# Products of zeros on TensorE while the tokens are chosen: 40 in layer 0, 110 in layer 1

## The chip, the cores and the metric

One core of a Trainium2 chip runs the whole program, so there is one span and one TensorE clock to look at. The metric is device time in microseconds of one execution, the median over several. [...]

## What is computed

Two layers of a diffusion backbone on 1024 latent tokens and, in layer 0, 256 context tokens, 1024 wide, in float32. Each layer has a mixer (windowed attention and spatial gating in layer 0, latent attention and a short convolution in layer 1) and then a feed-forward with 16 experts that choose their tokens:

```python
def expert_choice_ffn(h, w_router, w1, w3, w2):
    n_tok, d = h.shape[1], h.shape[2]
    cap = EC_FACTOR * n_tok // N_EXPERTS
    aff = jax.nn.softmax(jnp.einsum('bnd,de->bne', h, w_router).astype(jnp.float32), axis=-1)
    gate, idx = lax.top_k(jnp.swapaxes(aff, 1, 2), cap)
    xs = jax.vmap(lambda hb, ib: hb[ib])(h, idx)
    a = jnp.einsum('becd,edf->becf', xs, w1)
    b = jnp.einsum('becd,edf->becf', xs, w3)
    y = jnp.einsum('becf,efd->becd', jax.nn.silu(a) * b, w2) * gate[..., None].astype(h.dtype)
```

The choice is a top 128 of 1024 for each expert. No expert can start before the affinities of the last tokens are known, ranked, merged, turned and used to gather rows.

## The kernel before, in words

Every float32 product is three float16 products of high and low halves (`mm3`, L141 to L143). The weights come from memory as 1 MB slabs, `raw`; ScalarE writes the high half (L100) and VectorE the low one (L101) into `spl`.

The mixer of a layer is written as streams that `weave` mixes. Its last stage is `tail`, for 128 tokens at a time: the output projection `yps`, the norm, the router's logits `lg` (L319), a softmax, and a transposition of the affinities into `affps` (L333), which VectorE copies to `aff` (L334).

The choice is `topk` on VectorE: 16 rounds of MAX8, MATCH_REPLACE8 and FIND_INDEX8 (L350, L354, L356) on the last 384 tokens; the first 640 are ranked earlier, beside other work. `merge` joins the two lists (L368 to L372, the last writes `tkir`), `slots` turns indices and gates on TensorE into `slps` (L382, L384), VectorE copies them (L385, L386), and GpSimd's queue then gathers the rows `xs` of expert 0 (L488). In `experts` TensorE transposes `xs` into `tr` (L155), ScalarE and VectorE scale and split them into `xsh` and `xsl`, and the first expert products `pa`, `pb` follow. Ahead of those, TensorE makes two broadcasts of the modulation, `bcps` (L259), and in layer 0 `m5ps` (L509) and the context rows `trc` (L481).

In layer 0, `mods1` runs after the mixer's streams. It makes the first modulation bank of layer 1: nine groups of products `modps` on slabs `mslab`, a VectorE copy of the bank (L212), four transpositions `tr<-mod` and small VectorE operations (L234, L235). It shares the two buffers `za` in PSUM with the last tile of the mixer. A product of zeros is already there: `mod_bank` opens its bank with one (L193), on the tile `zero16`.

A scheduler sets the order of the instructions on every engine: it simulates the program with costs of its own and gives an engine, each time it is free, something that is ready in that simulation. On the chip each engine then goes through its list in that order. `issue_after(ins)` says that what is in it may be placed only after `ins`; it adds no wait of its own on the chip. `high_priority` puts something ahead of what else is ready.

Of the kernel before, what the change touches and what calls it, by code (L numbers as in the profile page):

```python
# [22 lines left out]
P = 128  # L23
# [3 lines left out]
NE = 16  # L27
# [26 lines left out]
def weave(*streams):  # L54


    live = [[st[0], 0.0, float(st[1]), st[2] if len(st) > 2 else 0.0, None] for st in streams]
    while live:
        s = min((v for v in live if v[4] is None or v[4]()), key=lambda v: v[3] + v[1] / v[2])
        try:  # L60
            r = next(s[0])
            s[4] = r if callable(r) else None
            s[1] += 0.0 if callable(r) else r
        except StopIteration:
            live.remove(s)
# [12 lines left out]
class Net:  # L78
# [61 lines left out]
    def mm3(self, ps, lh, ll, rh, rl, first, last):  # L140
        self.T.matmul(ps, lh, rh, start=first, stop=False)  # L141
        self.T.matmul(ps, lh, rl, start=False, stop=False)  # L142
        return self.T.matmul(ps, ll, rh, start=False, stop=last).ins  # L143

    def turn(self, dst, src):

# [136 lines left out]
    def tail(self, l, j, t, src, catT, wout, m2, xd, h2d, aff, psum, c4, t2, cn=None, xin=None, ptr=None):  # L283

        V, S, T = self.V, self.S, self.T
        ra, rb = self.RT[l, j]
        x = xin
        if x is None:
            x = c4([P, D], "xres")
            self.G.dma_start(x, src)  # L290
        for h in range(2):
            ps = psum([P, 512], "yps")
            for k in range(8):
                ch, cl = catT(k)
                wh, wl = wout(k, h)
                self.mm3(ps, ch, cl, wh, wl, k == 0, k == 7)
                if k % 2:
                    yield 1.3
            sl = slice(h * 512, (h + 1) * 512)
            if m2 is None:  # L300
                V.scalar_tensor_tensor(x[:, sl], ps, IS, x[:, sl], op0=OP.mult, op1=OP.add)
            else:
                tmp = t2([P, 512], "ytmp")
                V.tensor_tensor(tmp, ps, m2[:, sl], OP.mult)
                V.tensor_tensor(x[:, sl], x[:, sl], tmp, OP.add)
        self.G.dma_start(xd[t * P:(t + 1) * P, :], x)
        ptr = ptr or psum
        xn = (cn or c4)([P, D], "xn2")
        r = self.stats(x, D, xn, "t")
        hs = []  # L310
        for h in range(2):
            ps, = self.trans(x[:, h * 512:(h + 1) * 512], 4, ptr)
            hT = t2([P, 4, P], "h2T")
            S.activation(hT, ps, AF.Copy)
            hs.append(hT)
            yield 0.5
        lg = ptr([P, NE], "lg")
        for k in range(8):
            T.matmul(lg, hs[k // 4][:, k % 4], ra[:, k], start=(k == 0), stop=(k == 7))  # L319
        e = self.small.tile([P, NE], F32, name="re", bufs=2)  # L320
        V.scalar_tensor_tensor(e, lg, r, rb, op0=OP.mult, op1=OP.add)
        nm = self.small.tile([P, 1], F32, name="rnm", bufs=2)
        V.tensor_reduce(nm, e, axis=AX.X, op=OP.max, negate=True)
        den = self.small.tile([P, 1], F32, name="rden", bufs=2)
        self.last_exp = S.activation(e, e, AF.Exp, bias=nm, accum_out=den).ins
        V.reciprocal(den, den)
        V.tensor_scalar(e, e, den, None, op0=OP.mult)
        pt = ptr([P, P], "affps")
        r0, cols = aff[1](t)
        if r0:  # L330
            T.matmul(pt[r0:r0 + NE, :], e, self.ident, start=True, stop=True, tile_position=(0, r0))
        else:
            T.transpose(pt[:NE, :], e, self.ident)  # L333
        V.tensor_copy(aff[0][r0:r0 + NE, cols], pt[r0:r0 + NE, :])  # L334
        S.activation(xn, x, AF.Copy, scale=r)
        self.G.dma_start(h2d[t * P:(t + 1) * P, :], xn)
        yield 1.0
# [295 lines left out]
    def even(self, xd, xdc, h2d, h2dc, then):  # L633
        nc, tc, V, S, T, G, Y, I = self.nc, self.tc, self.V, self.S, self.T, self.G, self.Y, self.I
        with self.pool("m0") as pm, self.pool("m0p", PSUM) as pp:
            za, zc = Tag(pp, "za", BK0[0]), Tag(pp, "zc", BK0[1])
# [212 lines left out]
            K = {}  # L849

            for t in range(NT):
                lo, hi = max(t - 1, 0), min(t + 1, NT - 1)
                n = hi - lo + 1
# [53 lines left out]
            def mods1():  # L907

                tags = itertools.cycle(range(4))
                pw = then()  # L910
                yield from self.mod_bank(1, 0, zq, lambda shape, name: pw.tile(list(shape), F32, name=name, tag=f"w{next(tags)}", bufs=1), (K["turn"], None), 2048)
                with tc.issue_after(K["turn"]):
                    self.first_slabs(0, 0, 7)
                self.split_first(0, 4, self.last_exp)
                self.mod_AB(1, 1, zq)

            pend = []

# [62 lines left out]
    def odd(self, ms, mw, xs, xsc, xd, h2d, W, then):  # L981
        nc, tc, V, S, T, G, Y, I = self.nc, self.tc, self.V, self.S, self.T, self.G, self.Y, self.I
# [8 lines left out]
        if True:  # L991
# [111 lines left out]
            K = {}  # L1103
# [5 lines left out]
            with self.pool("m1zp", PSUM) as pz:  # L1109
# [57 lines left out]
                if True:  # L1167
# [89 lines left out]
                    def att_all():  # L1257

                        for n in range(8 * NT):
                            t, h = n // 8, n % 8  # L1260
                            pTs = K.pop(("p", t, h))
                            for i in range(len(KB)):
                                pend.append((t, h, i, pTs[i]))
                                for c in SP[i]:
                                    if n + LA < 8 * NT:
                                        score((n + LA) // 8, (n + LA) % 8, c)
                                        yield 0.6
                                if len(pend) > AB[3]:
                                    values()
                                    yield 0.3  # L1270
                            done.add(("h", t, h))
                            if h == 7 - LA and t + 1 < NT:
                                yield after(("q", t + 1))
                        while pend:
                            values()
                        for p in (mt, m1, ap):
                            p.__exit__(None, None, None)
                        then()
                        pools.append(self.pool("m1ap2", PSUM))
                        pq = pools[-1].__enter__()  # L1280
                        K["z"] = Tag(pq, "y", 4), Tag(pq, "tr", 2)
                        self.first_slabs(1, 0, FS)
                        done.add("att")

                    def q_all():
                        for t in range(1, NT):
                            yield after(("h", t - 1, 0))
                            yield from Q(t)
                            done.add(("q", t))
# [35 lines left out]
                    def choose():  # L1325
                        yield after(("c", NR1 // P - 1))
                        aff_t = K["aff"]
                        yield from self.topk(aff_t[:, :NR1], NR1, CAP, "r")
                        yield after(("c", NT - 1))
                        with tc.high_priority():  # L1330
                            yield from self.topk(aff_t[:, NR1:], 1024 - NR1, CAP, "l", NR1, aff_t[:, :1024 - NR1], 1)

                    def splits():
                        yield after("att")
                        for i in range(11):
                            yield lambda: len(self.ahead) > i
                            yield 1.0
                            if i in PL:
                                self.split_first(i, i + 1)
                            else:  # L1340
                                raw, _ = self.ahead[i]
                                sp = self.spl()
                                for h in range(2):
                                    hs = slice(h * 1024, (h + 1) * 1024)
                                    self.split_w(raw[:, hs], sp[:, 0, hs], sp[:, 1, hs])
                                self.ahead[i] = raw, sp

                    weave((Q(0), 4))
                    for h in range(LA):
                        for i in range(3):  # L1350
                            score(0, h, i)
                    weave((self.first(att_all(), HP[0]), 29), (q_all(), 6, 0.1), (tails(), CV), (self.first(choose(), HP[2]), 10, TS), (splits(), SPR, 8.6))
                    with tc.high_priority():
                        r = self.slots(*self.merge(self.tk["r"], self.tk["l"]), CAP, zc, False)
                for p in reversed(pools):
# [126 lines left out]
```

## Time and profile before

| | us |
|---|---|
| median of 3 runs | 2637.35 |
| lowest and highest | 2634.41, 2641.68 |
| the profiled execution's own time | 2632.11 |
| its span, first to last instruction | 2630.0 |
| TensorE (PE) busy, share of the span | 2329.2, 89% |
| VectorE (DVE) busy | 1997.7, 76% |
| ScalarE (ACT) busy | 1696.7, 65% |
| mean granted clock of TensorE | 0.943 |

Times in the rows are microseconds from the span's start. In a timeline a row is: start, busy time, engine, line, operation, tile written and tiles read, shapes, count, and in brackets the engine's idle time before it and what ended it. PEld is TensorE's weight load, which lies beside the products. A product's busy time is longer than its distance to the next one, since products are pipelined. The layer 0 choice of tokens lies between 607 and 636 us, layer 0's experts from 646 to 1330 us, the choice of layer 1 between 1997 and 2025 us, and its experts from 2039 us to the end.

### The profile page before, as it was taken

Reading aid. Unit: us, or ns where it says so; the run is one execution under the profiler, and the core shown is the slowest. Engines: PE = TensorE matmul, PEld = TensorE weight load, DVE = VectorE, ACT = ScalarE, POOL = GpSimd, SP = SyncE. Lnnn points to the kernel's source line nnn. Section 1 sums busy time; section 2 is a strip of 40 time slices with the busy share of each in tenths; the row PEclk is TensorE's granted clock in tenths of the full one; section 3 lists DMA queues with packets and bytes.
Section 4 is the critical chain, followed back from the end, with each engine's and each line's share of the span. In section 5 each row is a group of like instructions: output and inputs, shape, how many; then the busy total and the mean of one; then the engine's idle time right before and its main releaser. Section 6 shows DMA issues by size and latency. Waiting matters only on the chain. (4 is left out here: it accounts for less than half of the span.)

```text
span 2630.0 us, 48132 instructions
## 1 busy us (share of the span) xinstructions
PE 2329.2 (89%) x19023; PEld 1415.0 (54%) x19023; DVE 1997.7 (76%) x3586; ACT 1696.7 (65%) x2748; POOL 320.6 (12%) x196
## 2 busy tenths in 40 slices
PE   6889998867999999999969999978982999999995
PEld 2335555543877778786836555535541444444442
DVE  5546767787887788777848687788796889888887
ACT  4434666535777787777726466567655777777774
POOL 1000000003111111111310000000025011112120
PEclk9999999877999999999989999989985999999998
DMA  8783555548998989888967577788866899999997
GB/s 321 192 213 84 134 104 116 123 126 312 352 337 324 328 328 325 327 320 300 326 187 203 119 143 143 133 151 184 176 175 272 311 364 395 368 360 367 361 363 274
DMA packets 461705, 660.25 MB, mean 251 GB/s; under 512 B 371083, under 2 KB 371387, under 8 KB 410789
## 3 DMA queue, kind: packets, MB, share of 16 engines
q1 hardware_dynamic: 439894, 582.81, 69.7%
q0 software_dynamic: 21584, 74.37, 9.8%
q8 instruction: 149, 2.44, 0.4%
q14 instruction: 78, 0.64, 0.1%
HBM read 525.82 MB, written 41.94 MB: 216 GB/s over the span
## 5 line engine op out<-in xcount | busy, mean ns | idle before, releaser
L101 DVE SCALAR_TENSOR_TENSOR spl<-raw,spl 128x2048 f16<-128x2048 f32 x369 | 834.6, 2285 | 167.3 <-ACT spl L100 166.5
L100 ACT ACTIVATE spl<-raw 128x2048 f16<-128x2048 f32 x369 | 693.5, 1911 | 166.4 <-DMA raw<-in_w 109.5
L141 PE MATMUL pa<-xsh,spl 128*128 128x160 f16 x1024 | 214.6, 233 | 2.3 <-ACT xsh L112 2.3
L143 PE MATMUL pb<-xsh,spl 128*128 128x160 f16 x1024 | 214.6, 233 | 0.5 <-DVE spl L101 0.5
L142 PE MATMUL pa<-xsl,spl 128*128 128x160 f16 x1024 | 214.7, 233 | 0.3 <-DVE xsl L114 0.3
L143 PE MATMUL pa<-xsh,spl 128*128 128x160 f16 x1024 | 214.7, 233 | 0.0
L142 PE MATMUL pb<-xsl,spl 128*128 128x160 f16 x1024 | 214.6, 233 | 0.0
L141 PE MATMUL pb<-xsh,spl 128*128 128x160 f16 x1024 | 214.5, 233 | 0.0
L141 PEld LDWEIGHTS <-spl 128*128 128x128 f16 x2048 | 200.6, 98 | 8.9 <-issue 8.0
L141 PE MATMUL y<-spl,gh 128*128 128x512 f16 x512 | 195.2, 384 | 9.0 <-ACT gh L112 8.4
L143 PEld LDWEIGHTS <-spl 128*128 128x128 f16 x2048 | 200.8, 98 | 1.1 <-DVE spl L101 0.7
L142 PEld LDWEIGHTS <-spl 128*128 128x128 f16 x2048 | 200.8, 98 | 0.3
L143 PE MATMUL y<-spl,gl 128*128 128x512 f16 x512 | 190.1, 386 | 11.4 <-DVE gl L114 11.3
L142 PE MATMUL y<-spl,gh 128*128 128x512 f16 x512 | 195.6, 382 | 1.8 <-DVE spl L101 1.8
L594 POOL DMA_INDIRECT xd<-ysb,idxl x31 | 113.2, 3652 | 532.3 <-DVE ysb L587 508.2
L1218 ACT ACTIVATE pr<-sps,nm 128x512 f32<-128x512 f32 (+1 forms) x192 | 116.7, 611 | 88.3 <-DVE nm L1209 67.7
L141 PE MATMUL po<-vS,pT 128*128 128x64 f16 x976 | 118.0, 198 | 49.1 <-DMA pT<-ps 32.5
L1201 PE MATMUL sps<-kT,qT 128*128 128x512 f16 (+1 forms) x576 | 134.4, 355 | 12.3 <-ACT pr L1218 11.9
L114 DVE TENSOR_TENSOR ps<-pr,ps 128x512 f16<-128x512 f32 (+1 forms) x192 | 112.2, 595 | 38.9 <-ACT ps L112 38.3
L141 PEld LDWEIGHTS <-pT 128*128 128x128 f16 x976 | 92.1, 101 | 82.8 <-DMA pT<-ps 46.5
L1202 DVE TENSOR_REDUCE mx<-sps 128x1 f32<-128x512 f32 (+1 forms) x192 | 112.8, 595 | 26.2 <-PE sps L1201 24.9
L208 PE MATMUL modps<-mslab,cs 128*2 128x512 f32 x384 | 88.5, 690 | 33.6 <-DMA mslab<-in_mod_w 28.7
(431 smaller groups left out, 5883.8 us busy)
## 6 DMA issues: line engine op xcount, KB each, us to landing
raw<-in_w SPq DMA_DIRECT2D x384, 1024.0 KB, 6.8
mslab<-in_mod_w SPq DMA_DIRECT2D x80, 512.0 KB, 4.8
mslab<-in_mod_w SPq DMA_DIRECT2D x8, 1024.0 KB, 8.2
raw<-in_wz SPq DMA_DIRECT2D x12, 512.0 KB, 6.4
raw<-in_wconv SPq DMA_DIRECT2D x24, 256.0 KB, 3.8
xin<-in_x POOLq DMA_DIRECT2D x8, 512.0 KB, 4.8
raw<-in_ev_wo SPq DMA_DIRECT2D x8, 512.0 KB, 6.9
xres<-in_x POOLq DMA_DIRECT2D x8, 512.0 KB, 5.4
```

What stands on the lines that cost most here:

```text
L100: self.S.activation(hi, raw, AF.Copy, scale=scale)
L101: self.V.scalar_tensor_tensor(lo, raw, scale, hi, op0=OP.mult, op1=OP.subtract)
L114: return self.V.tensor_tensor(lo, src, hi, OP.subtract)
L141: self.T.matmul(ps, lh, rh, start=first, stop=False)
L142: self.T.matmul(ps, lh, rl, start=False, stop=False)
L143: return self.T.matmul(ps, ll, rh, start=False, stop=last).ins
L208: T.matmul(ps[c0:c0 + 2], lhs, slab[:rows, g * 512:(g + 1) * 512], start=False, stop=(k == 8), tile_position=(0, c0))
L594: G.indirect_dma_start(out=xd, out_offset=IOA(ap=lat[0][:, e:e + 1], axis=0), in_=ysb, in_offset=None, compute_op=OP.add)
L1201: T.matmul(ps[:, :w], qT[:, 4 * j + h % 4], kT[:, k, c0:c0 + w], start=j == 0, stop=j == 2)
L1202: V.tensor_reduce(mx[:, i:i + 1], ps[:, :w], axis=AX.X, op=OP.max)
L1218: S.activation(pr[:, :w], sp[i][:, :w], AF.Exp, bias=nm, scale=SC1, accum_out=dn[:, i:i + 1])
```

## The change

A new helper, `idle`, writes n products of a 128 x 128 block of zeros with a 128 x 512 block of zeros into one PSUM tile that nobody reads. It may be placed only after the transposition of the last affinities, `last_aff`, which `tail` now keeps.

```diff
+    def idle(self, psum, n, ins):
+
+        ps = psum([P, 512], "idle")
+        with self.tc.issue_after(ins):
+            for i in range(n):
+                self.T.matmul(ps, self.zero16[:, 0:1].broadcast_to([P, P]), self.zero16[:, 0:1].broadcast_to([P, 512]), start=i == 0, stop=i == n - 1)
...
-            T.transpose(pt[:NE, :], e, self.ident)
+            self.last_aff = T.transpose(pt[:NE, :], e, self.ident).ins
...
                 self.split_first(0, 4, self.last_exp)
                 self.mod_AB(1, 1, zq)
+                self.idle(za, 40, self.last_aff)
...
+                    self.idle(K["z"][0], 110, self.last_aff)
                     with tc.high_priority():
                         r = self.slots(*self.merge(self.tk["r"], self.tk["l"]), CAP, zc, False)
```

In layer 0 the call stands at the end of `mods1`, behind the choice in the program's text; in layer 1 it stands just ahead of `merge` and `slots`. Where the products land on TensorE is the scheduler's doing. The lines of the changed kernel are 7 to 9 higher than those of before; L150 is the product of zeros.

**TensorE at the end of layer 0's choice, before.** `mod` is the modulation bank, `tkir` the merged indices, `tkvr` the gates, `xc` and `xs` gathered context and latent rows.

```order
L208 MATMUL modps<-mslab,one_77 2x512 x4
L155 MATMUL tr<-c_ident,mod_6688 128x128 x4
L382 MATMUL slps<-c_ident,tkir 128x16
L384 MATMUL slps<-c_ident,tkvr 128x16
L259 MATMUL bcps<-mod_990,c_ident 128x512 x2
L509 MATMUL m5ps<-mod_990,c_ident 32x512 x2
L481 MATMUL trc<-c_ident,xc 128x32 x8
L155 MATMUL tr<-c_ident,xs 128x128 x12
```

The same place in the changed kernel:

```order
L162 MATMUL tr<-c_ident,mod_6688 128x128 x4
L150 LDWEIGHTS zero_75
L150 MATMUL idle<-zero_75 128x512
...
L389 MATMUL slps<-c_ident,tkir 128x16
L391 MATMUL slps<-c_ident,tkvr 128x16
L150 LDWEIGHTS zero_75
L150 MATMUL idle<-zero_75 128x512
...
L266 MATMUL bcps<-mod_990,c_ident 128x512 x2
L516 MATMUL m5ps<-mod_990,c_ident 32x512 x2
L162 MATMUL tr<-c_ident,xs 128x128 x4
L488 MATMUL trc<-c_ident,xc 128x32 x8
```

Of the 40 products of zeros 19 now stand between the bank's transpositions and `slps`, and 21 between `slps` and `bcps`; `trc` has moved behind the first four transpositions of `xs`. VectorE's list has the same order there in both kernels, with the bank's copy behind the last round of the ranking.

**TensorE at the choice of layer 1, before.** `re` are affinities, `xx` the residual rows.

```order
L155 MATMUL tr<-c_ident,xx 128x128 x8
L319 MATMUL lg<-ra_18928,h2T 128x16 x8
L333 MATMUL affps<-c_ident,re 16x128
L382 MATMUL slps<-c_ident,tkir 128x16
L384 MATMUL slps<-c_ident,tkvr 128x16
```

And in the changed kernel:

```order
L326 MATMUL lg<-ra_18969,h2T 128x16 x8
L340 MATMUL affps<-c_ident,re 16x128
L150 LDWEIGHTS zero_75
L150 MATMUL idle<-zero_75 128x512
...
L389 MATMUL slps<-c_ident,tkir 128x16
L391 MATMUL slps<-c_ident,tkvr 128x16
```

All 110 stand between the last affinities and `slps`.

**SyncE's queue in layer 1's experts, before**: the loads of one expert in the later part of the stage, `w1` and `w3` for the first products, `w2` for the second.

```order
L447 DMA raw_29230<-in_w1 128x2048
L447 DMA raw_29245<-in_w3 128x2048
L447 DMA raw_29235<-in_w1 128x2048
L447 DMA raw_29240<-in_w3 128x2048
L447 DMA raw_29338<-in_w2 128x2048
L447 DMA raw_29343<-in_w2 128x2048
L447 DMA raw_29348<-in_w2 128x2048
L447 DMA raw_29419<-in_w1 128x2048
L447 DMA raw_29353<-in_w2 128x2048
```

And in the changed kernel:

```order
L454 DMA raw_29382<-in_w1 128x2048
L454 DMA raw_29387<-in_w1 128x2048
L454 DMA raw_29397<-in_w3 128x2048
L454 DMA raw_29392<-in_w3 128x2048
L454 DMA raw_29490<-in_w2 128x2048
L454 DMA raw_29495<-in_w2 128x2048
L454 DMA raw_29500<-in_w2 128x2048
L454 DMA raw_29505<-in_w2 128x2048
L454 DMA raw_29571<-in_w1 128x2048
```

Nothing was written for this place; the scheduler's simulation went another way after the added products. The four loads of `w2` now come together, and the two of `w1` ahead of those of `w3`. The scheduler also exchanged neighbours on every engine in layer 1's mixer and experts, and a few in layer 0's experts.

## Rows read from the trace of the kernel before

**Rows 1.** The page's slices: granted clock of TensorE in 40 slices of 65.75 us.
```profile
PEclk9999999877999999999989999989985999999998
```
**Rows 2.** Timeline of layer 0 around the end of its choice.
```profile
633.38 0.67 DVE L212 COPY mod<-modps 128x512 f32<-128x512 f32 x1
634.11 1.12 PE L155 MATMUL tr<-c_ident,mod 128*128 128x128 f32 x4 [6.52 <-DVE mod L212]
...
634.94 0.28 DVE L372 TENSOR_TENSOR tkir<-mg_m,tkil 16x128 f32<-16x128 f32 x1
...
635.28 0.28 PE L382 MATMUL slps<-c_ident,tkir 16*128 16x16 f32 x1
...
635.60 3.78 PE L259 MATMUL bcps<-mod,c_ident 128*128 128x512 f32 x4
...
636.26 0.98 POOL L488 DMA_INDIRECT xs<-h,idxl  x1 [7.37 <-DVE gatel L386]
...
641.00 1.09 PE L155 MATMUL tr<-c_ident,xs 128*128 128x128 f32 x8
...
645.81 0.23 PE L141 MATMUL pa<-xsh,spl 128*128 128x160 f16 x1 [2.32 <-ACT xsh L112]
```
**Rows 3.** Landing of the gathers of xs between 630 and 650 us, from its tile's view.
```profile
DMA to landing us min/median/max: 4.4/5.2/6.1
```
**Rows 4.** Line L193, the products of zeros already there: ns shortest/median/longest, first and last.
```profile
L193 PE MATMUL modps<-zero x6: 376/500/634, 0.9 to 1411.7; 128*128 128x512 f16 x6
```
**Rows 5.** Timeline of layer 1 from the last affinities to the first expert products.
```profile
1996.92 0.37 PE L333 MATMUL affps<-c_ident,re 128*16 128x128 f32 x1 [7.95 <-DVE re L327]
...
2024.93 0.28 PE L382 MATMUL slps<-c_ident,tkir 16*128 16x16 f32 x1 [27.64 <-DVE tkir L372]
...
2025.67 3.49 PE L259 MATMUL bcps<-mod,c_ident 128*128 128x512 f32 x4 [0.35 <-DVE gatel L386]
...
2034.21 1.94 PE L155 MATMUL tr<-c_ident,xs 128*128 128x128 f32 x8 [5.04 <-DMA xs<-h,idxl]
...
2039.10 0.61 PE L141 MATMUL pa<-spl,xsh 128*128 128x512 f16 x1 [2.95 <-ACT xsh L112]
...
2039.93 0.63 PE L141 MATMUL pb<-spl,xsh 128*128 128x512 f16 x1
...
2040.36 0.63 PE L142 MATMUL pb<-spl,xsh 128*128 128x512 f16 x1
...
2042.45 0.38 PE L143 MATMUL pa<-spl,xsl 128*128 128x512 f16 x1
...
2042.67 0.38 PE L141 MATMUL pa<-spl,xsh 128*128 128x512 f16 x1
```
**Rows 6.** Stretches: length, busy of PE, PEld, DVE, ACT, POOL, clock, DMA share, GB/s.
```profile
625.87:639.52 13.65, 7.08 (x20) 2.37 (x14) 9.91 (x40) 7.54 (x5) 4.77 (x4) 0.50 0.70 256
646.35:649.76 3.41, 3.23 (x25) 3.22 (x25) 1.15 (x3) 2.10 (x5) 0.00 (x0) 0.50 0.70 216
2028.75:2032.16 3.41, 0.42 (x1) 0.00 (x0) 0.00 (x0) 0.60 (x1) 3.13 (x2) 1.00 0.85 322
2032.16:2042.40 10.24, 5.24 (x16) 2.77 (x17) 4.07 (x5) 3.69 (x5) 2.85 (x2) 0.50 0.48 159
...
650.00:1320.00 670.00, 655.56 (x7787) 526.83 (x7785) 540.33 (x426) 499.52 (x616) 111.74 (x57) 1.00 0.90 323
```
**Rows 7.** Waits of TensorE between 645 and 1330 us, the longest kind: total us, times, longest.
```profile
PE y L143 <- DVE gl L114: 6.6, 12, 0.7
```
**Rows 8.** The chain that ended last, in layer 1's experts: transpositions of xs, once an expert.
```profile
2234.69 0.87 PE tr L155 x8
...
2266.43 0.87 PE tr L155 x8
...
2439.78 0.87 PE tr L155 x8
...
2477.43 0.87 PE tr L155 x8
```

## The prediction

> **What bounds the kernel now.** I read the clock slices first, to see where TensorE runs at the lower clock. In the page's 40 slices the clock is full nearly everywhere; it dips in layer 0's mixer, at the change of layers (slice 21) and around the choice of layer 1 (slices 30 and 31) [rows 1]. The change is about two of these places, so next I read the timeline around each of them, to see who waits for whom.
>
> In layer 0 VectorE is the bound up to the choice: its copy of the modulation bank starts at 633.38, right behind the ranking, TensorE's transpositions of the bank wait for it and start at 634.11, and the merged indices start at 634.94. TensorE turns the indices at 635.28, so at that moment it is idle by hundredths only: the transpositions end at 634.11 + 1.12 = 635.23. After it come the broadcasts from 635.60, the gather of expert 0's rows issued at 636.26, their transpositions at 641.00, and the first expert products at 645.81 [rows 2]. From there TensorE is the bound: it is busy for 655.56 of 670.0 us, at full clock throughout [rows 6], and its longest kind of wait sums to 6.6 us [rows 7].
>
> In layer 1 the choice is VectorE's alone: the last affinities are done on TensorE at 1996.92 + 0.37 = 1997.29, and it stands idle for 27.64 us until the merged indices come, at 2024.93. Then the broadcasts take 3.49 us, the gathered rows end a wait of 5.04 us at 2034.21, and the first expert products start at 2039.10 [rows 5].
>
> **Layer 1: 110 products of zeros in the gap.** A 128x512 product costs its distance to the next: 2040.36 - 2039.93 = 0.43 us at half clock, 2042.67 - 2042.45 = 0.22 us at full clock [rows 5]. The six products of zeros that are there already last 376 to 634 ns [rows 4], as products of data do at the two clocks (0.38 and 0.63 us, [rows 5]); I take zeros at the same price. Weight loads lie beside the products. The nearest dense run that starts at half clock begins at 2039.10 and is at 0.38 us a product from 2042.45, so 3.3 us; I take that for the zeros, 8 products, and 102 at 0.216: 3.4 + 22.0 = 25.4 us, from 1997.3 to 2022.7. The indices come at 2024.93, so nothing waits; 2.2 us are to spare. The bounds: all at full clock, 23.8 us; all at half clock, 110 x 0.427 = 47.0 us, to 2044.3, which is 19.4 us late.
>
> What does the higher clock bring? The broadcasts get some 1.7 us shorter, but the transpositions behind them wait for the gather, so that gives nothing. The first expert products would gain if the clock lasted until them. The trace of before answers this: the clock stood at 1.00 from 2028.75 to 2032.16, after the broadcasts, and at 0.50 from 2032.16 to 2042.40, while TensorE waited for the gather and the split and then began the products [rows 6]. Zeros ahead of the indices lie before that wait, not in it, so the products start at half clock as now. Layer 1 gives 0; if they did start at full clock, half of 2042.4 - 2039.1 = 3.3 us, 1.7 us, would be gained, and I keep that for the range.
>
> **Layer 0: 19 products ahead of the indices.** These stand behind the bank's transpositions, which end at 635.23, and ahead of the indices' transposition, which was ready at that very moment [rows 2]. Nothing hides them. The clock there is 0.50 from 625.87 to 639.52 [rows 6]. With 3.3 us at half clock, 8 products, and 11 at 0.216, they take 3.4 + 2.4 = 5.8 us (bounds 19 x 0.216 = 4.1 and 19 x 0.427 = 8.1). Indices, copies and the gather's issue are late by that.
>
> **Layer 0: 21 products behind them.** They run while the gather is under way, but the broadcasts and the context's transpositions stand behind them. From 635.60 to 641.00 TensorE had 5.4 us of such work before it turned the rows. At full clock the 3.78 us of broadcasts halve, so 3.5 us remain. The zeros take 21 x 0.216 = 4.5 us. TensorE is then done at 635.6 + 5.8 + 4.5 + 3.5 = 649.4, against 641.00: 8.4 us late. The gather, issued at 636.26 + 5.8 = 642.1 and landing 5.2 us later [rows 3], is there at 647.3, so TensorE decides. Bounds: with the fewest zeros at half clock (4.1) and 2.6 added behind, 6.7 us; with all at half clock, 8.1 + 9.0 = 17.1 us. I take 8.4, as dense runs do raise the clock.
>
> The first products of layer 0's experts then start near 654. They began at half clock: 25 products in the 3.41 us from 646.35 [rows 6], worth 1.7 us if the clock were full. Between the rows' transpositions and the products there is a wait of 2.32 us [rows 2], and in the trace the clock fell in it; I take it to fall again, so 0, and keep 1.7 for the range. Behind, TensorE has no slack but its own waits, 6.6 us for the largest kind in 12 pieces [rows 7], most inside an expert; I let 1 us be absorbed. The stage's delay of 7.4 us passes into layer 1, whose first work needs the sum of all experts.
>
> **What moves besides.** The loads of layer 1's experts are issued in another order, and neighbours change places on all engines there and in its mixer. Nothing is added, so the price is only in waits. The scale is in the chain: an expert takes 2266.43 - 2234.69 = 31.7 us in one part of the stage and 2477.43 - 2439.78 = 37.7 us in another [rows 8], 5.9 us apart by order and waits alone. A gain or a loss of one such expert either way is what I allow in the forecast; the value is 0, since both orders keep the same work on each engine.
>
> **Sum.** 0 (layer 1) + 8.4 - 1 (layer 0) + 0 = 7.4, say 7 us slower. The profiled execution would go from 2632.11 to 2639; its span is 2630.0. That execution is 5.2 us under the median of 2637.35, and the same difference on the median gives **2644 us**, 0.27% slower. A measurement of this kernel can tell some 0.3%, 7.9 us, from no change, so the forecast lies just inside that.
>
> **The rivals.**
> *Zeros don't lift the clock (slower).* If products of zeros left the clock at 0.50, layer 0 would lose the upper bound of 17.1 us, and layer 1's 47.0 us would hold the indices back by 19.4: with 1 us absorbed 35.5 us, 2673. It turns slower from where zeros at half clock fill more than 27.64 us, 65 of them. For it: no row shows a run of zeros. Against: the single ones last as long as other products [rows 4]. [...] Chance 0.08.
> *The order costs more.* Two more experts at 37.7 instead of 31.7, 11.8 us, on top of 7: 2656. Chance 0.10, slower.
> *The clock is kept.* The waits ahead of both layers' first products are too short for the clock to fall, and each layer gains 1.7 us; with zeros at full clock (6.7 instead of 8.4) and 1 us absorbed the sum is 6.7 - 1 - 3.4 = 2.3: 2640, no change. For it: in layer 0 the wait is 2.32 us only. Against: the clock fell in both places now. [...] Chance 0.15.
> *The new order of loads is the better one (faster).* Three experts that now take 37.7 us take 31.7: 17.7 gained, 7 lost, 2626.7. For it: TensorE uses both `w1` before `w3` late in the stage, and the new order brings them so. It decides from 15 us of gain. Chance 0.12, of which 0.10 is faster and 0.02 no change.
>
> **How the numbers follow.** The forecast has 0.55. It lies 1 us inside the bound with some 6 us of the order's scatter around it, so 0.27 is no change and 0.28 slower. No change: 0.27 + 0.15 + 0.02 = 0.44. Slower: 0.28 + 0.08 + 0.10 = 0.46. Faster: 0.10. The range goes from 2633 (the kept clock and one expert's 5.9 us gained) to 2657 (the order's loss); it leaves out the faster rival and the clock that zeros don't lift, 2 in 10.
>
> **What would show it.** In layer 0: `idle` products between the bank's transpositions and `slps`, TensorE busy up to `slps`, and `slps` 5 to 6 us behind the merged indices, which didn't wait before; the first `pa` some 8 us later than now against the choice's end. In layer 1: `slps` ended by the merged indices, not by `idle`, and the first `pa` still at 0.43 us a product. It would be wrong if `slps` of layer 0 came at once, if a clock of 1.00 stood at either first `pa`, or if the stage of layer 1's experts were over 6 us shorter or longer.

## The result, and the profile after

The changed kernel takes 2666.07 us (median of 4 runs, 2661.51 to 2670.05) against 2639.51 of the kernel before on the same chip (4 runs, 2634.41 to 2642.19): a ratio of 1.0093, 95% interval 1.0077 to 1.011, so 20 to 29 us slower. The direction was forecast; the size is over three times the forecast's 7 us, and the time lies 9 us above the range.

The changed kernel's page has the granted clock, in tenths of full speed, in 40 slices of 66.5 us; against [rows 1] only five slices differ: 3 and 4 in layer 0's mixer, and 30 to 32 around layer 1's choice, where slice 31, with the 110 products in it, goes from 5 to 8.

```profile
PEclk9988999877999999999989999989978899999998
```

The timeline of layer 0 around the end of its choice, in the changed kernel (start, us, engine, line, operation, what ended the idle time before):

```profile
637.32 1.12 PE L162 MATMUL tr<-c_ident,mod 128*128 128x128 f32 x4 [5.78 <-DVE mod L219]
...
638.15 0.28 DVE L379 TENSOR_TENSOR tkir<-mg_m,tkil 16x128 f32<-16x128 f32 x1
638.23 6.54 PE L150 MATMUL idle<-zero 128*128 128x512 f16 x19
...
644.70 0.23 PE L389 MATMUL slps<-c_ident,tkir 16*128 16x16 f32 x1
...
644.92 4.76 PE L150 MATMUL idle<-zero 128*128 128x512 f16 x21
645.20 2.28 DVE L101 SCALAR_TENSOR_TENSOR spl<-raw,spl 128x2048 f16<-128x2048 f32 x1
645.48 2.86 POOL L495 DMA_INDIRECT xs<-h,idxl  x1 [13.39 <-DVE gatel L393]
...
654.95 0.65 PE L162 MATMUL tr<-c_ident,xs 128*128 128x128 f32 x4 [2.24 <-DMA xs<-h,idxl]
...
660.98 0.29 PE L141 MATMUL pa<-xsh,spl 128*128 128x160 f16 x1 [3.07 <-ACT xsh L112]
```

The indices are ready at 638.43 and are turned at 644.70: 6.3 us that did not exist before, the 19 products [rows 2]. The 21 behind them take 4.76 us, at the full clock (1.00 from 644.92 to 649.68). But the transpositions of the rows end a wait for the gather, not for TensorE: the gather's issue took 2.86 us instead of 0.98, beside a VectorE split that now falls on the same moment. Two things make it fall there: in the changed order ScalarE's half of that split stands ahead of the copies of the broadcasts, where the old order has it between them, and with the zeros it had long ended (641.25) when `slps` came. Without the zeros the same order has the split at 643.67, clear of the gather's issue at 640.06.

The timeline of layer 1 from the zeros to the first products, changed kernel:

```profile
2031.34 26.23 PE L150 MATMUL idle<-zero 128*128 128x512 f16 x110
...
2056.79 4.06 POOL L441 TENSOR_TENSOR spl<-raw,spl 128x2048 f16<-128x2048 f32 x1 [2.02 <-ACT spl L440]
2057.05 3.94 DVE L375 TENSOR_TENSOR mg_m<-tkvr,tkvl 16x128 f32<-16x128 f32 x1
...
2062.85 0.28 PE L389 MATMUL slps<-c_ident,tkir 16*128 16x16 f32 x1 [5.29 <-DVE tkir L379]
...
2063.59 3.78 PE L266 MATMUL bcps<-mod,c_ident 128*128 128x512 f32 x4 [0.35 <-DVE gatel L393]
2063.73 2.87 POOL L495 DMA_INDIRECT xs<-h,idxl  x1 [2.88 <-DVE gatel L393]
...
2077.46 0.63 PE L141 MATMUL pa<-spl,xsh 128*128 128x512 f16 x1
2077.89 0.63 PE L142 MATMUL pa<-spl,xsh 128*128 128x512 f16 x1
```

The 110 products end at 2057.57 and `slps` waits another 5.29 us for VectorE: they are hidden. In that wait the clock falls again: it is 1.00 up to 2062.70 and 0.50 from 2062.80 to 2075.78. The broadcasts take 3.78 us at 0.50, no better than the 3.49 of [rows 5]; the four of layer 0 take 1.98 at 1.00 (from 649.75). The first products are still 2077.89 - 2077.46 = 0.43 us apart.

So the places that the forecast speaks of carry some 12 us. For the rest I cut the kernel into six stages: layer 0's choice (last affinities to the first `pa`), its experts (to the last `ysb`), layer 1's mixer in two parts (to the first `sps`, with the low-rank projections; then to the last affinities), layer 1's choice, its experts. The windows of the changed kernel (columns as in [rows 6]):

```profile
609.99:660.98 50.99, 33.33 (x149) 10.29 (x150) 32.03 (x102) 27.62 (x29) 22.72 (x9) 0.70 0.67 250
660.98:1350.04 689.06, 674.31 (x7884) 537.43 (x7887) 544.09 (x435) 503.00 (x623) 108.20 (x57) 0.99 0.88 315
1350.04:1527.67 177.63, 148.22 (x1137) 95.09 (x1129) 121.76 (x468) 80.91 (x228) 12.01 (x16) 0.91 0.67 179
1527.67:2031.17 503.50, 439.47 (x3761) 250.24 (x3762) 385.23 (x974) 321.02 (x740) 28.85 (x21) 0.93 0.76 159
2031.17:2075.78 44.61, 32.50 (x125) 14.45 (x126) 33.82 (x91) 22.42 (x17) 29.18 (x9) 0.81 0.61 246
2075.78:2631.93 556.15, 536.05 (x2552) 253.82 (x2552) 481.79 (x311) 430.48 (x411) 83.12 (x29) 0.99 0.97 366
```

The same stages in a second profile of the kernel before, taken later (the first is of an execution 5 us under the median):

```profile
610.77:649.83 39.06, 22.68 (x108) 5.86 (x109) 32.03 (x102) 27.33 (x29) 21.77 (x9) 0.67 0.83 312
649.83:1339.82 689.99, 673.00 (x7884) 536.33 (x7887) 544.57 (x435) 502.47 (x623) 105.15 (x57) 1.00 0.88 316
1339.82:1513.57 173.75, 147.21 (x1136) 94.72 (x1129) 119.88 (x468) 80.95 (x228) 11.30 (x16) 0.92 0.69 184
1513.57:2011.46 497.89, 434.71 (x3761) 248.12 (x3762) 384.89 (x974) 327.51 (x744) 32.96 (x22) 0.93 0.78 167
2011.46:2053.55 42.09, 6.08 (x16) 3.10 (x16) 30.67 (x91) 17.43 (x13) 25.10 (x8) 0.54 0.49 192
2053.55:2616.55 563.00, 539.90 (x2552) 255.06 (x2552) 482.10 (x311) 430.03 (x410) 87.30 (x29) 0.98 0.96 361
```

Stage by stage the change is +11.9, -0.9, +3.9, +5.6, +2.5 and -6.9 us. These sum to 16 us of the 26.6, since this second profile is of an execution 9 us over the median of its runs and the changed kernel's of one 5 us under; against the first profile the stages are +12.0, +3.2, +5.9, +10.0, +2.4 and -7.0. Layer 1's mixer and experts, where nothing was added, move by several us each. What they have that is new is the scheduler's other order; the experiments below put it to the test.

### The profile page after: what moved, and what is told of

Read it like the earlier page. It is cut to its first block, busy times and chain, and to the rows that moved or that the text cites. A ratio compares the mean times of both kernels' runs of the same rounds, so it can differ in the third digit from the quotient of the medians.

```text
span 2659.6 us, 48426 instructions
## 1 busy us (share of the span) xinstructions
PE 2381.4 (90%) x19173; PEld 1440.0 (54%) x19173; DVE 2004.1 (75%) x3586; ACT 1697.0 (64%) x2748; POOL 312.2 (12%) x196
## 4 chain that ended last, share of the span: by engine, by line
PE 48%; DMA 17%; DVE 15%; issue 10%; ACT 9%; POOL 0%; SPq 0%; DVEq 0%; POOLq 0%; ACTq 0%
DMA raw<-in_w 5%; DVE spl L101 5%; DMA pT<-ps 3%; ACT spl L100 3%; PE pa L142 3%; PE pa L143 3%; PE pa L141 3%; PE y L143 3%; PE pb L141 2%; PE pb L142 2%; PE pb L143 2%; PE y L142 2%; PE y L141 2%; PE sps L1209 2%; PE modps L215 2%
```

## The experiments

Two edits made behind the scheduler separate what a plain rewrite can't. Each run is compared with the kernel before on its own chip. One keeps the changed kernel's order on every queue and cuts chosen products of zeros, with their weight loads, to 4 columns, so that they take next to no time:

```diff
+def shrink(nc, names):
+    cut = lambda a: copy.replace(a, ap=[a.ap[0], [0, 4]])
...
+                if x.name in names:
+                    w, o = b.instructions[ld], x.outs[0]
+                    b.instructions[ld] = copy.replace(w, ins=[cut(w.ins[0])])
+                    o = copy.replace(o, ap=[[o.ap[0][0], 4], [1, 4]])
+                    b.instructions[k] = copy.replace(x, ins=[cut(a) for a in x.ins], outs=[o])
...
+    shrink(nc, set(net.idles[0:150]))
```

The other keeps the order of the kernel before and puts products of zeros into it by hand (step counts TensorE's products from `slps`):

```diff
+def add_zeros(nc, plan):
...
+                        new.append(copy.replace(zl, name=f"I-9{c:03d}00", sync_info=None))
+                        new.append(copy.replace(zm, name=f"I-9{c:03d}01", outs=[out], sync_info=None, start_tensor_calc=True, stop_tensor_calc=True))
...
+    add_zeros(nc, {0: ((-1, 19), (1, 21)), 1: ((-1, 110),)})
```

My theory from these stages was that about half of the loss is layer 0's zeros and half the order; the rival, that the zeros do it all.

### The changed order, with and without zeros

All products cut (`net.idles[0:150]`):

> The changed kernel with every instruction in its place on every queue, but each of the 150 products of zeros (and its weight load) cut to 4 columns, so that they take next to no time: the order alone. Theory A (about 12 us of the change's 25 come from the zeros of layer 0, the rest from the order that the scheduler wrote differently, the zeros of layer 1 cost nothing): 2652 us (2648 to 2656), 10 to 16 us over the kernel before; in layer 0 the first slps within 2 us of the kernel before, layer 1's experts start some 15 us later beyond what layer 0 lost. Theory R (the order is worth nothing, the zeros of both layers cost all 25): 2640 us, within 4 of the kernel before.

Measured: 2661.55 us against 2641.78, ratio 1.0074 (1.0059 to 1.0089), 16 to 24 us slower. The order alone costs more than I allowed, 20 us, and the rival falls. Beside the order this run keeps the PSUM tiles that the products claim and the 150 short products; ahead of layer 0's `slps` these take 0.3 us. Two runs further down tell the tiles from the order: with both tiles and another order layer 0 and the low-rank stage last as before, and with layer 1's tile alone nothing is lost.

Layer 0's cut, layer 1's whole (`[0:40]`):

> The changed kernel in its own order, layer 0's 40 products cut to 4 columns, layer 1's 110 whole. Theory A: layer 1's zeros end 5 us before slps can start and hold nothing, so within 3 us of the run with all of them cut (about 2652). Theory R: half or more of the 25 us are layer 1's, so 2650 to 2655 against 2640 of the run with all cut, 10 or more apart.

Measured: 2660.91 us, ratio 1.0074 (1.006 to 1.0088), the same as with all cut. Layer 1's 110 products cost nothing in this order that six runs can tell.

Layer 1's cut, layer 0's whole (`[40:150]`):

> The changed kernel in its own order, layer 0's 40 products whole, layer 1's 110 cut to 4 columns. Theory A: as the changed kernel within 3 us (2663 to 2669); without the zeros the clock at layer 1's slps is half as before, and it is half with them too by the time of the first products, so nothing is lost. Theory R: the zeros of layer 1 carry half of the cost or more, so 10 or more under the changed kernel, 2652 to 2656.

Measured: 2666.09 us, ratio 1.01 (1.008 to 1.0119), as the whole change. Layer 0's 40 products seem to add some 5 us to the order's 20, but from two sets of six runs that scatter by 14 us each this alone is not clear of noise (2 us less to 12 more).

Only layer 0's 20 behind `slps` cut (`[19:39]`):

> The changed kernel in its own order, layer 1's 110 products whole and layer 0's first 19 whole (those ahead of slps); of the 21 behind slps 20 are cut to 4 columns. Theory G (behind slps the gather decides: its issue takes 2.9 us instead of 1.0 beside a VectorE split, and the 21 zeros lie in its wait): within 2 us of the changed kernel (2664 to 2668), the first products of the experts 15 to 17 us behind slps as in the changed kernel (16.3). Theory T (TensorE decides there, as the prediction had it): the first products 5 to 8 us sooner, 2657 to 2661.

Measured: 2669.23 us, ratio 1.0104 (1.0087 to 1.0121): no gain over the 2666.09 with all 40, as theory G has it. The two runs with zeros ahead of layer 0's `slps`, taken together, are 3 to 11 us slower than the two without, all on one chip, so in this order layer 0's zeros do have a price. The timeline shows the gather deciding:

```profile
645.60 0.23 PE L389 MATMUL slps<-c_ident,tkir 16*128 16x16 f32 x1
...
646.38 2.86 POOL L495 DMA_INDIRECT xs<-h,idxl  x1 [13.37 <-DVE gatel L393]
...
655.79 1.11 PE L162 MATMUL tr<-c_ident,xs 128*128 128x128 f32 x4 [6.07 <-DMA xs<-h,idxl]
```

The rows are turned 655.79 - 645.60 = 10.2 us behind `slps`; with the 21 products whole it is 654.95 - 644.70 = 10.3. What they took on TensorE only shortens its wait for the gather, 2.24 us with them and 6.07 without.

Where the order's 20 us are, the stages of the run with all products cut tell:

```profile
610.35:653.27 42.92, 25.68 (x148) 8.46 (x149) 32.13 (x102) 27.40 (x29) 20.83 (x9) 0.62 0.82 299
653.27:1348.87 695.60, 674.97 (x7884) 536.23 (x7887) 544.69 (x435) 502.54 (x623) 104.13 (x57) 0.99 0.87 312
1348.87:1534.07 185.20, 151.62 (x1136) 95.62 (x1129) 121.94 (x468) 80.98 (x228) 11.97 (x16) 0.88 0.69 172
1534.07:2040.15 506.08, 438.06 (x3761) 249.95 (x3762) 385.39 (x974) 320.92 (x740) 28.81 (x21) 0.93 0.75 158
2040.15:2085.02 44.87, 9.21 (x125) 5.94 (x125) 33.80 (x91) 22.41 (x17) 29.17 (x9) 0.54 0.61 249
2085.02:2639.07 554.05, 533.49 (x2552) 253.29 (x2552) 481.70 (x311) 428.88 (x408) 99.53 (x29) 0.99 0.97 366
```

Against the second profile of before: +3.9 and +5.6 in layer 0, +11.5 and +8.2 in layer 1's mixer, +2.8 at its choice, and -9.0 in its experts. All five profiles in the changed order have the low-rank stage (layer 1's mixer up to the first `sps`) at 177.6 to 186.0 us; all seven in the old order at 170.4 to 173.8. Layer 1's experts are 554.1 to 557.0 us in the one and, leaving out the kernel whose clock was kept, 562.3 to 563.5 in the other. In the low-rank stage TensorE's waits name a part of the loss: the products of the key and value projections, which have other neighbours in TensorE's list, stand waiting for a transposed load. That row in the kernel before (second profile) and with the order alone:

```profile
PE kvps L141 <- DMA ckT<-hk: 3.0, 2, 2.3
```

```profile
PE kvps L141 <- DMA ckT<-hk: 9.1, 2, 8.6
```

That gives 6 of the 11.5 us; the wait is 4.5 to 10.5 us in all five profiles of the changed order and at most 3.2 in the seven of the old one. The clock is 0.92 in the stage before and 0.88 here. In the attention that follows it is again a wait for a transposed load, that of the probabilities; before (second profile) and with the order alone:

```profile
PE po L141 <- DMA pT<-ps: 33.4, 29, 3.4
```

```profile
PE po L141 <- DMA pT<-ps: 39.4, 39, 3.2
```

It sums to 38.0 to 42.2 us in the five profiles and to 32.4 to 34.9 in the seven. Which exchange makes the loads late or their readers early was not tried by itself.

### The old order, with zeros put in by hand

First, what does a second profile of the kernel before look like?

> The kernel before once more, for a second profile: its first one (2634.4 us) is 7 us under the median of its runs. 2636 to 2648; which stage carries the difference tells how far the stages of two profiles can be compared: up to 4 us before layer 0's choice and up to 8 in layer 1's low-rank stage are expected, the rest within 2 each.

2646.35 us, 9 over the median of that batch; span 2644.3, 14 us over the first profile's 2630.0, and the stages differ by 4 us each in layer 0's mixer and experts and in layer 1's attention, by 2 in the low-rank stage. So a single stage of a single profile is known to about 4 us, and a difference is relied on here only where it holds over all profiles of an order.

All 150 products in the old order:

> The kernel before with the order of every queue as it was, and the same 150 products of zeros put in by hand behind the scheduler: 19 between layer 0's tr(mod) and slps, 21 behind slps, 110 behind layer 1's last affps (they write to banks that are idle there). Theory A (order 20 us, zeros of layer 0 5, zeros of layer 1 nothing; the numbers of the four runs before this one): 2647 us (2644 to 2652), 3 to 10 over the kernel before; the first products of layer 0's experts 8 to 12 us later, and half of that given back in the experts' waits for slabs. Rival (the zeros cost little only because the changed order is slow in layer 0's experts anyway): 10 to 12 over, 2652 to 2654, with nothing given back.

Measured: 2657.74 us against 2636.97, ratio 1.0071 (1.0048 to 1.0095), 13 to 25 us slower. Theory A, with 3 to 10, falls: in the order of before, the same products cost as much as the order alone did in the other. The rival said 10 to 12 with nothing given back; the measured time is above that too. The timeline of layer 0:

```profile
644.11 0.23 PE L382 MATMUL slps<-c_ident,tkir 16*128 16x16 f32 x1
...
644.34 4.76 PE L193 MATMUL modps<-zero 128*128 128x512 f16 x21
...
644.89 0.98 POOL L488 DMA_INDIRECT xs<-h,idxl  x1 [13.37 <-DVE gatel L386]
...
652.93 1.56 PE L155 MATMUL tr<-c_ident,xs 128*128 128x128 f32 x12 [0.52 <-ACT m L260]
...
657.92 0.23 PE L141 MATMUL pa<-xsh,spl 128*128 128x160 f16 x1 [3.43 <-ACT xsh L112]
```

Here the gather's issue takes 0.98 us and the rows are not waited for: TensorE decides, as the prediction had it. The stage of the choice is 657.92 - 609.42 = 48.5 us against 39.0 before, +9.5, and layer 0's experts (688.8 us, against 685.8 and 690.0 in the two profiles of before) give nothing back that can be told.

Layer 0's 40 products alone, in the old order (`{0: ((-1, 19), (1, 21))}`):

> The kernel before in its own order, with layer 0's 40 products alone put in by hand (19 ahead of slps, 21 behind), none in layer 1. Theory B (in the old order the 40 cost 6.2 us at slps and 3.3 at the first products, nothing is given back, layer 1's cost nothing): 8 to 13 us over the kernel before, ratio 1.003 to 1.005. Theory C (what the run with all 150 showed beyond that, 19 us in all, belongs to layer 1's 110): the same 8 to 13 here, but the run with all 150 stays 5 or more above it. Theory D (the rest was the spread of that batch): this one 12 to 19.

Measured: 2658.63 us against 2641.25, ratio 1.0065 (1.0044 to 1.0086), 12 to 23 us slower, the same as with layer 1's 110 beside them. Theory C falls: layer 1's products have no price here either. The time is in theory D's range, above B's. Of the 17 us the stage of the choice has 48.5 - 39.0 = 9.5.

The 19 alone, then the 21 alone:

> The kernel before in its own order, only the 19 products ahead of slps put in. They delay slps by 6.2 us and raise the clock; behind slps the four bcps run at the full clock (1.9 us instead of 3.8) and tr(xs) then waits for the gather: first products 5.5 to 6.5 us later, total 4 to 9 us over the kernel before. If the delay is taken up by the experts' waits for slabs: 0 to 3.

Measured: 2652.45 us, ratio 1.0036 (1.0021 to 1.0052), 6 to 14 us slower. The timeline:

```profile
638.18 6.54 PE L193 MATMUL modps<-zero 128*128 128x512 f16 x19
...
644.87 1.98 PE L259 MATMUL bcps<-mod,c_ident 128*128 128x512 f32 x4
...
649.92 1.06 PE L155 MATMUL tr<-c_ident,xs 128*128 128x128 f32 x8 [1.47 <-DMA xs<-h,idxl]
```

`slps` is 6.2 us late; behind the zeros the broadcasts take 1.98 us instead of 3.78, and the first products are 5.0 us late (a stage of 44.0 us against 39.0).

> The kernel before in its own order, only the 21 products behind slps put in. They start at the half clock: 21 x 0.43 = 9.0 us if it holds half all the way, some 6 us if it rises on the way as it did in the changed kernel after 12 products or so; then bcps at the full clock (1.9). tr(xs), at 5.7 us behind slps before, comes at 9 to 12: first products 4 to 7 us later, total 3 to 9 us over the kernel before. If the gather's wait hides them: 0 to 2.

Measured: 2649.65 us, ratio 1.0028 (1.0014 to 1.0042), 4 to 11 us slower; the 21 took 6.64 us (4.76 where they stand behind the 19), the broadcasts behind them 1.88, and the stage 44.3 us, +5.2. Each half of layer 0's zeros has its price, and within their intervals the two add up.

### Which layer draws the order

Layer 1's 110 alone, scheduled by itself (the `idle` call in layer 0 left out):

> The change with layer 1's 110 products alone, scheduled by itself: its order differs from that of the kernel before in about 2% of TensorE's rows, where the whole change differs in 7%. Theory A (it is layer 0's 40 that make the scheduler write layer 1 differently, and the 110 hide in a wait): 2642 us (2638 to 2647). Theory R (the 110 have a price, or bring the slow order themselves): 2650 or more.

Measured: 2637.96 us against 2636.97, ratio 0.9997 (0.9982 to 1.0012): no difference. So it takes the 40 products in layer 0 for the scheduler to write the order that costs; whether they do it without the 110 was not tried.

All products written with 4 columns from the start, so that the scheduler counts little for them:

> The change with all 150 products written with 4 columns from the start, so that the scheduler counts next to nothing for them and draws a third order (6% of TensorE's rows differ from the kernel before, 7% from the changed one). If the changed kernel's order is slow because of one place in it, this one is near the kernel before, 2640 to 2646; if the kernel before simply has a good order and any other draw is worse (theory L), 2648 to 2665, with the loss again in layer 1's mixer.

Measured: 2652.02 us against 2636.97, ratio 1.0047 (1.003 to 1.0063), 8 to 17 us slower, with layer 0's choice, its experts and the low-rank stage as before (40.0, 687.9 and 171.9 us) and layer 1's attention at 505.5 against 493.5 to 497.9. The wait for the transposed probabilities is 38.1 us here, as in the changed order. So two other orders lose, only partly in the same places, and there is no one bad place. But theory L's "any other draw is worse" goes too far: the order with layer 1's 110 alone is another draw as well, though nearer to the kernel before, and loses nothing.

### Keeping the clock to the first products

The old order, nothing in layer 0; in layer 1 zeros also in the two waits behind `slps` (`{1: ((-1, 110), (3, 26), (11, 8))}`), as the one way seen to a gain:

> The kernel before in its own order, layer 0 without products of zeros; layer 1 with 110 behind the last affps, 26 behind bcps (the wait for the gather) and 8 behind tr(xs) (the wait for xsh), so that the clock is full at the first products of the experts. If it is, their pitch is 0.22 instead of 0.43 us, tr(xs) takes 1.1 instead of 1.9, and first products and first two experts together end 2 to 5 us sooner; the whole 2 to 5 us under the kernel before (ratio 0.998 to 0.9995), at the edge of what five rounds tell. If loads and splits set the first experts: no difference beyond the 0.8 of tr(xs).

Measured: 2640.34 us against 2641.25, ratio 1.0005 (0.999 to 1.0019): no difference that can be told. The timeline and the last stage:

```profile
2031.39 5.85 PE L193 MATMUL tr<-zero 128*128 128x512 f16 x26
2038.29 1.07 PE L155 MATMUL tr<-c_ident,xs 128*128 128x128 f32 x8 [1.04 <-DMA xs<-h,idxl]
2039.19 1.91 PE L193 MATMUL tr<-zero 128*128 128x512 f16 x8
2042.72 0.39 PE L141 MATMUL pa<-spl,xsh 128*128 128x512 f16 x1 [1.62 <-ACT xsh L112]
2042.95 0.38 PE L142 MATMUL pa<-spl,xsh 128*128 128x512 f16 x1
```

```profile
2042.72:2601.01 558.29, 535.31 (x2552) 253.49 (x2552) 481.90 (x311) 429.10 (x410) 87.51 (x29) 0.99 0.96 364
```

The clock is kept: products 0.23 us apart instead of 0.43, and the experts' stage 558.3 us where the six other profiles in this order have 562.3 to 563.5. The 4 to 5 us are there in the profile; the runs, whose interval reaches from 3 us faster to 5 slower, don't confirm them.

## Why the prediction was right or wrong

**Layer 1's zeros, forecast 0.** Right, to within the some 4 us that the runs can tell: with the 110 products and without, in the changed order (1.0074 both), alone (0.9997), and in the old order (1.0071 with, 1.0065 without). They took 26.2 us for the 25.4 of the sum. The clock was lost behind them, as the sum took it: in the changed kernel already ahead of `slps` (0.50 from 2062.80, `slps` at 2062.85).

**Layer 0's 19 products, forecast 5.8.** Right: 6.2 to 6.3 us at `slps`.

**Layer 0's 21 products, forecast 2.6 more.** The sum said that the gather is there at 647.3, "so TensorE decides". In the old order that is what happens, and the size is near: the first products 9.5 us late for the 8.4 of the sum; the 1 us that it let the experts absorb behind them doesn't show. In the changed order the step fails: the transpositions of the rows moved ahead of the context's, and the gather, late by the 19 products, is issued beside a split and takes 2.86 us (in the same order without zeros ahead it takes 0.98); so the gather decides. The first products came 11.9 us late, and the zeros behind `slps` cost nothing. The forecast's 7.4 lies within the 3 to 11 us that layer 0's zeros add in this order, but that is luck, as the wait that it worked out is not the one that decided.

**The order, valued at 0 with one expert's 5.9 us either way: this is the step that failed.** "Since both orders keep the same work on each engine" is true of the busy times and was no bound on the waits. The order alone costs 20 us (16 to 24). The scale was read from one stage, layer 1's experts, where the new order does win, 7 us; between the profiles without zeros in layer 0 (two in this order, three in the old one) it loses 9 to 15 in the low-rank stage, 5 to 13 in the attention that follows, some 3 at layer 1's choice and 9 to 14 in layer 0's choice and experts, which the forecast did not look at. One of its own signs of being wrong came true here: layer 1's experts over 6 us shorter. The price had to be sought in every stage in which a queue's rows change, and no row of before that the forecast used gives its sign.

**The two do not add up.** Order 20 and zeros 17 to 19 by themselves, 25 together (20 to 29). In the changed order without zeros TensorE comes to layer 0's experts 8 us earlier than in the changed kernel and then waits more: choice and experts together last 42.9 + 695.6 = 738.5 us there, 51.0 + 689.1 = 740.1 in the changed kernel. In the old order the same sum is 39.1 + 690.0 = 729.1 without zeros and 48.5 + 688.8 = 737.3 with them. Over all profiles the sum is 725 to 729 in the old order without zeros there, 738 in the changed one, and 737 to 743 in both once layer 0's zeros are in: the old order loses 8 to 15 by them, the changed one 2 to 5. This places the overlap of the two prices in layer 0.

**What stays open.** In the old order the zeros cost 17 us; the choice shows 9.5, choice and experts of layer 0 together 8 to 15. In the four profiles with zeros in layer 0 layer 1's attention is also longer, 498.9 to 503.1 us against 493.5 to 497.9 in the three without, though order and work there are the same. No run tells why.

**The rivals.** Zeros that don't lift the clock: no, 21 of them took 4.76 us and 110 took 26.2. The zeros are 0.43 us apart at first and 0.22 later; among the 110 the granted clock averages 0.56 up to 2036.00 and is 1.00 from there to their end. The kept clock: not in layer 1 of the changed kernel, nor in layer 0, whose first products are at half clock too (0.50 from 660.98 to 664.00). But the prediction misread layer 0 of the kernel before. It took the clock to fall in the wait ahead of the first products; the first four still came at the full clock, and it fell behind them. In the old order with the 19 products alone it did not fall there at all. Before, and that run at the place that [rows 6] show at 0.50:

```profile
645.81:646.35 0.54, 0.44 (x4) 0.30 (x4) 0.54 (x1) 0.30 (x1) 0.00 (x0) 1.00 1.00 425
```

```profile
654.49:657.90 3.41, 3.23 (x47) 3.23 (x47) 1.14 (x3) 2.11 (x5) 0.00 (x0) 1.00 0.70 238
```

So in layer 0 of that run the clock was kept behind the zeros, 47 products in the time of 25; the run was slower all the same. The better order of loads: it is better, by 7 us in layer 1's experts, not the 17.7 of that rival. The order that costs more had the sign and, at 2656, most of the time; its 11.8 us were placed in the one stage that got faster.

## What to carry to other kernels

Where a scheduler writes the order, an added instruction can have two prices, its own time and that of the redrawn order (17 to 19 us and 20 here); cut it to nothing in the scheduled program, and put it by hand into the old one, and each is measured. The filler that ended 5.29 us ahead of the `slps` that was being waited for (layer 1's 110) cost nothing that the runs can tell; the one in front of a ready `slps` (layer 0's 19, 6.54 us) delayed it by 6.2 to 6.3 us. The clock that was raised ahead of one last wait was lost in that wait in layer 1 (0.50 from 2062.80) and lasted beyond the waits with the 19 alone in layer 0 (1.00 from 654.49 to 657.90). Two orders of the same work differ here by 20 us in 2640, so a redrawn order is an unknown with a range in every stage it touches, not a zero.

## What the runs showed of the hardware

A tiny VectorE operation took 3.94 us beside a GpSimd one of 4.06. `mg_m`, 16x128, takes 0.28 us as its neighbours do (`tkir` at 638.15), but 3.94 in layer 1 of the changed kernel, where GpSimd's split of a slab began 0.26 us ahead of it and took 4.06: they end together, at 2060.99 and 2060.85. This is 3.7 us on the path to layer 1's `slps`, of which the stage shows some 2.5: it lasts 44.5 to 45.0 us in all five profiles of the changed order and 41.8 to 42.5 in the seven of the old. The other way round, the gather's issue on GpSimd takes 0.98 us alone and 2.86 where VectorE's split started 0.28 us before it; it ends at 648.34, 0.86 behind the split's end. The kernel before has the same in layer 1 (2.89 us, the split 0.28 ahead of it). What makes the one last as long as the other, in either place, no run here shows.
